# S5 states through two PSUM banks, readouts in trace order, an earlier 1/rms and tables split by use, in a two-layer hybrid block

## The chip, the core and the metric

The kernel runs on one core of a Trainium2 chip. The metric is the device time of one execution in microseconds (us). A core has five engines with an instruction stream each: PE (TensorE, matrix products and transposes), DVE (VectorE), ACT (ScalarE), POOL (GpSimd) and SP (SyncE, which here only issues transfers). The engines run side by side and wait for one another through semaphores. PE writes into PSUM, a small memory of eight banks; the other engines empty these banks into SBUF, the working memory.

## The reference, cut to what matters

512 latent tokens and 256 context tokens, 1024 channels wide, go through two layers. Each layer is

```
h     = modulate(x, sh1, sc1);  hc = modulate(ctx, ...)    # shift and scale from silu(c) @ w_mod[l]
proj  = h @ w_in[l]             # keys, values, latent keys, u of S5, queries, three gates
ya    = grouped-query attention (8 heads of 64, 2 key heads), rms-normed q and k, rotary
yc    = latent attention: cq = rms_norm(proj[..., C_Q]); qc = cq @ c_w_qb; keys, values = ckv @ c_w_kvb
ys    = S5: states s[t] = abar * s[t-1] + bbar @ u[t] (complex, 32 groups of 64 states, forward and
        backward over the tokens), y = Re(C s) + d * u, gelu, gated linear unit
mix   = (sigmoid(g0)*(ya@Wa) + sigmoid(g1)*(ys@Ws) + sigmoid(g2)*(yc@Wc)) @ w_out
x     = layer_norm(alpha*x + g1*mix);  then a squared-ReLU MLP of 4096 with a modulation and a norm
```

The context tokens take the same way in layer 0; in layer 1 only their keys, values and S5 states are needed. All results are float32.

## The kernel before

**Products.** A float32 operand is split into a high part, rounded to the matrix format, and a low part (the rest). A product is three matmuls: high x high, low x high, high x low (`mm3`, L167 to L169). For weights a DMA brings the raw tile (`wr`), ACT casts the high part `wh` (L151), and DVE subtracts to get `wl` (L124). These three lines carry most of PE's time.

**The stages of a layer**, in time: the modulated input; projections, which run beside a part of the gates (sigmoids of `h @ w_in`, blocks of 128 columns); the chunk states of S5; attention of both kinds, beside which a "filler" runs (gates, the S5 readouts, the last gates); the merge of the three branches; `w_out` and the norm; the MLP. Beside the MLP of layer 0 run the tables and the modulation of layer 1. Beside the merge of layer 0 runs the rest of layer 0's own modulation (`mods(l, (5,))`): 16 loads `wm` of 256 KB, which DVE multiplies and adds into `acc` (L309), a sum by PE, and a small DMA.

**S5.** The 768 tokens are cut into 96 chunks of 8. From the constants of a layer, `s5_tables` makes small matrices per group: `gb`, which PE transposes (L580) and which gives Q (input of a chunk to its end state), P (`pt`, state at a chunk's start to the chunk's outputs) and M (input to output within a chunk). They are written to memory (`Qd`, `Pd`, `Md`) and loaded again. `s5_states` forms the end states of all chunks: for each of 16 pairs of groups, a load `qp`, four matmuls `b<-u,qp` (L1027) into one PSUM bank, then three copies into `slots`, forward states and backward ones in turned order (L1030 to L1032). GpSimd then scans over the 96 chunks (L1040 to L1043). `s5_readout` takes eight quarter-steps of four groups each: loads `m` and two `qp` and, every second time, `u`; GpSimd copies the states of the groups to `bsl` (L1060 to L1063); PE does M times u (L1070) and P times states (L1073); ACT takes the bank to `y`. `m` and `bsl` have one buffer each, `qp` three in layer 0 and four in layer 1.

**Latent queries.** `compress(hf, ms)` makes the six 128-row blocks of `cq` for one half of the tokens, with the sum of squares in `acc`; `queries(hf)` sums `acc` over rows on PE (L832), takes 1/rms (`rstd_of`, L648 and L649), and multiplies by `w_qb`, with 1/rms as a factor when ACT empties the bank (L643).

**What sets the order.** The Python code is traced once. Generators that run side by side are drawn from in turn, by weights (`merge`, `mixed`); every instruction gets a priority by when it was traced, `later(gen, d)` adds to it, and a list scheduler with a simulated time line then fixes the order in each engine's stream. An engine runs its stream strictly in that order. All DMAs are issued from one queue, SP's (L78), in one order as well. `issue_after(i)` keeps what is traced inside it behind the instruction `i` on i's engine. A tile pool with n buffers hands out the same memory after n tiles, and the next user waits for the last reader of the old one.

Of the kernel before, what the change touches and what calls it, by code (L numbers as in the profile page):

```python
# [21 lines left out]
P = 128  # L22
# [47 lines left out]
class Block:  # L70
# [36 lines left out]
    def later(self, gen, d, behind=()):  # L107

        while True:
# [10 lines left out]
            yield v  # L120

# [404 lines left out]
    def s5_tables(self, pool, l, engs, G):  # L526
# [5 lines left out]
        for q in range(16 // G):  # L532
            tt = engs[q % len(engs)].tensor_tensor
# [30 lines left out]
            tt(out=gb[:, :, 1], in0=m1, in1=m2, op=ALU.add)
            yield 2.0
            pt = self.t(pool, [P, N, 2, 8, 16], F32, "pt")
            tt(out=m1, in0=pw(s["qr"]), in1=ch(ct[:, 0]), op=ALU.mult)
            tt(out=m2, in0=pw(s["qi"]), in1=ch(ct[:, 1]), op=ALU.mult)
            tt(out=pt[:, :, 0], in0=m1, in1=m2, op=ALU.subtract)
            nci = self.t(pool, [P, N, 16], F32, "nci")  # L570
            nc.vector.tensor_scalar(out=nci, in0=ct[:, 1], scalar1=-1.0, scalar2=None, op0=ALU.mult)
            tt(out=m1, in0=pw(s["qr"]), in1=ch(nci), op=ALU.mult)
            tt(out=m2, in0=pw(s["qi"]), in1=ch(ct[:, 0]), op=ALU.mult)
            tt(out=pt[:, :, 1], in0=m1, in1=m2, op=ALU.subtract)
# [9 lines left out]

            cb = self.t(pool, [P, N, 2, 2, 16], F32, "cb")
            nc.gpsimd.memset(cb, 0.0)
            for dr in range(2):
                hp = slice(dr * 64, dr * 64 + 64)
                nc.gpsimd.tensor_copy(cb[hp, :, 0, dr, :], ct[hp, 0])
                nc.gpsimd.tensor_copy(cb[hp, :, 1, dr, :], nci[hp])  # L590
# [110 lines left out]
    def projections(self, l, hT, pool, tp, per):  # L701
# [127 lines left out]
        def queries(hf):  # L829
# [5 lines left out]
            r = self.rstd_of(ps[:, :, 0], (8, nt), 96 * EPS)  # L835
# [23 lines left out]
        yield from compress(1, range(3))  # L859
        yield from queries(0)  # L860
        yield from compress(1, range(3, 6))
        yield from queries(1)
# [151 lines left out]
    def s5_states(self, sp, l, slots):  # L1014
# [4 lines left out]
        for gp in range(16):  # L1019
# [4 lines left out]
            ps = self.bank([P, 2, 2, NCH], which="gate")  # L1024
# [5 lines left out]
            nc.scalar.copy(sv[fw, :, :, 1:96], ps[fw, :, :, 0:95])  # L1030
            nc.scalar.copy(sv[bw, :, :, 1:33], ps[bw, :, :, 31::-1])
# [14 lines left out]
    def s5_readout(self, sp, l, slots):  # L1046
# [5 lines left out]
        for q in range(8):  # L1052
# [13 lines left out]
            for g in range(4):  # L1066
                if g % 2 == 0:
                    pt = self.t(sp, [P, 2, 2, P], F32, "qp")
                    self.dma(out=pt.rearrange("p g r c -> p (g r c)"), in_=self.Pd[l, q * 2 + g // 2])
# [471 lines left out]
```

## Time and profile before

| | |
|---|---|
| median of 3 runs | 2761.7 us (2759.91 to 2764.09) |
| the profiled execution | 2761.72 us, of which the instructions span 2759.9 us |
| mean granted clock of PE in it | 0.962 of full speed |
| busy: PE, DVE, ACT, POOL | 2570.2, 1794.7, 1197.2, 1167.4 us |
| DMA | 395.40 MB, mean 143 GB/s |

Line numbers (L1027) are lines of the kernel that the profile belongs to; the changed kernel's are 5 to 12 higher behind the first new function. A row of a group, "L1030 ACT COPY slots<-b x32: 787/817/866, 395.2 to 1942.3", gives engine, operation, what is written from what (by the names of the program), count, the shortest, median and longest duration in ns, and the first and last start in us. A row of the time line, "406.61 2.02 PE L1027 MATMUL b<-u,qp ... x8 [1.05 <-ACT slots L1032]", gives start and duration in us and in brackets how long the engine had stood still before it, and what ended that. A row of the waits, "PE b L1027 <- ACT slots L1032: 19.6, 24, 1.7", gives who waited for whom: the sum in us, the number of waits, the longest. In the table of stretches each engine has its busy time and its number of instructions; PEclk is the granted clock of PE, the mean over the stretch. A row of the transfers, "qp<-Qd SPq DMA_DIRECT2D x32, 256.0 KB, 3.0", ends with the median us from issue to landing.

In the order's listings below, a row is one instruction of one engine's stream: line, operation, output<-inputs with the program's names and buffer numbers, the shape, and a count where equal rows follow each other.

### The profile page before, as it was taken

To read this page: it belongs to the slowest core of one execution; us is meant where nothing else is said; L and a number is where in the kernel's file an instruction comes from. 1 tells how busy PE (TensorE), PEld (TensorE's weight loads), DVE (VectorE), ACT (ScalarE), POOL (GpSimd) and SP (SyncE) were. 2 spreads that over 40 slices of the span, in tenths; PEclk is the share of its full clock that TensorE was granted. 3 is DMA by queue.
4 is the path that set the end of the run, shared out by engine and by line. 5 is a ranking of instruction groups with operands and counts; after the bars stand their busy time and mean duration, and the time that the engine had idled before them with its cause. 6 is when DMAs were issued, how large, how long until landed. Compare 5 with 4: busy or idle time off the path is not lost.

```text
span 2759.9 us, 45140 instructions
## 1 busy us (share of the span) xinstructions
PE 2570.2 (93%) x16128; PEld 2380.6 (86%) x16128; DVE 1794.7 (65%) x3338; ACT 1197.2 (43%) x2420; POOL 1167.4 (42%) x1698
## 2 busy tenths in 40 slices
PE   7999998999899989999999988998998989799997
PEld 4989898999899878999999988997877868688886
DVE  7998535777778678456668574455766757844345
ACT  4333367655543235132322234457654633533332
POOL 2378313870202577445446361310785004722224
PEclk9989998999999999999999999999999989899999
DMA  8665666333464535334535256457433445433332
GB/s 242 203 191 154 173 180 178 109 98 114 156 197 127 197 124 172 98 101 141 151 111 157 90 160 175 118 152 209 131 100 118 136 149 176 137 108 106 107 100 84
DMA packets 485312, 395.40 MB, mean 143 GB/s; under 512 B 103624, under 2 KB 413128, under 8 KB 485088
## 3 DMA queue, kind: packets, MB, share of 16 engines
q1 hardware_dynamic: 485088, 392.53, 47.2%
q8 instruction: 127, 2.08, 0.3%
q14 instruction: 97, 0.79, 0.1%
HBM read 326.87 MB, written 70.67 MB: 144 GB/s over the span
## 4 chain that ended last, share of the span: by engine, by line
PE 62%; DVE 10%; POOL 10%; DMA 8%; ACT 4%; issue 4%; SPq 1%; POOLq 0%; DVEq 0%; ACTq 0%
PE b L168 17%; PE b L169 17%; PE b L167 17%; PE sc L872 3%; DVE acc L309 2%; DVE wl L124 2%; PE b L891 2%; DMA wm<-w_mod 2%; POOL slots L1043 1%; POOL sc L1040 1%; POOL sc L1042 1%; POOL sc L1041 1%; DMA wr<-w_in 1%; PE b L904 1%; PE b L903 1%
## 5 line engine op out<-in xcount | busy, mean ns | idle before, releaser
L151 ACT CAST wh<-wr 128x512 fp32r<-128x512 f32 (+1 forms) x672 | 410.0, 619 | 739.8 <-PE b L168 278.5
L124 DVE TENSOR_TENSOR wl<-wr,wh 128x512 fp32r<-128x512 f32 (+2 forms) x612 | 486.7, 807 | 293.4 <-ACT wh L151 282.7
L167 PE MATMUL b<-h,wh 128*128 128x384 f32 (+2 forms) x1712 | 597.4, 350 | 18.8 <-ACT wh L151 11.0
L169 PE MATMUL b<-h,wl 128*128 128x384 f32 (+2 forms) x1712 | 593.1, 347 | 7.8 <-DVE wl L124 7.6
L168 PE MATMUL b<-h,wh 128*128 128x384 f32 (+2 forms) x1712 | 594.7, 348 | 5.5 <-POOL h L393 4.4
L168 PE MATMUL b<-wl,a 128*128 128x256 f32 (+1 forms) x1460 | 446.9, 310 | 10.5 <-DVE wl L124 9.1
L169 PE MATMUL b<-wh,a 128*128 128x256 f32 (+1 forms) x1460 | 444.9, 308 | 0.0
L167 PE MATMUL b<-wh,a 128*128 128x256 f32 (+1 forms) x1460 | 438.4, 309 | 6.1 <-ACT a L643 3.8
L167 PEld LDWEIGHTS b<-h,wh 128*128 128x128 f32 x1712 | 327.6, 192 | 38.0 <-ACT wh L151 12.3
L169 PEld LDWEIGHTS b<-h,wl 128*128 128x128 f32 x1712 | 326.9, 191 | 27.9 <-DVE wl L124 12.2
L168 PEld LDWEIGHTS b<-h,wh 128*128 128x128 f32 x1712 | 327.4, 191 | 24.3 <-POOL h L393 6.0
L168 PEld LDWEIGHTS b<-wl,a 128*128 128x128 f32 x1460 | 280.0, 192 | 25.9 <-DVE wl L124 11.6
L167 PEld LDWEIGHTS b<-wh,a 128*128 128x128 f32 x1460 | 276.0, 192 | 22.5 <-ACT a L643 3.9
L1201 POOL TENSOR_TENSOR acc<-acc,tmp 128x256 f32<-128x256 f32 (+1 forms) x160 | 170.4, 1068 | 285.9 <-DVE tmp L1200 272.7
L169 PEld LDWEIGHTS b<-wh,a 128*128 128x128 f32 x1460 | 280.0, 192 | 12.5
L309 DVE SCALAR_TENSOR_TENSOR acc<-wm,silu,acc 128x512 f32<-128x512 f32 x236 | 194.6, 845 | 29.3 <-DMA wm<-w_mod 26.5
L1226 POOL TENSOR_TENSOR sq<-r 128x384 f32<-128x384 f32 (+2 forms) x102 | 99.0, 972 | 239.3 <-ACT r L1224 226.5
L1200 DVE TENSOR_TENSOR tmp<-b,bc 128x256 f32<-128x256 f32 (+1 forms) x160 | 77.2, 484 | 168.8 <-PE b L169 151.3
L894 DVE TENSOR_TENSOR pt<-b,pt 128x512 fp32r<-128x512 f32 x208 | 141.9, 685 | 33.2 <-ACT pt L893 31.7
L875 DVE TENSOR_REDUCE mx<-sc 128x1 f32<-128x768 f32 (+1 forms) x160 | 134.1, 844 | 34.3 <-PE sc L872 33.4
L167 PE MATMUL b<-a,wh 128*128 128x384 f32 (+1 forms) x384 | 131.2, 369 | 16.6 <-ACT a L1152 11.8
L878 ACT ACTIVATE p<-sc,mx 128x768 f32<-128x768 f32 (+1 forms) x160 | 131.5, 823 | 34.4 <-PE b L891 19.4
(377 smaller groups left out, 5138.8 us busy)
## 6 DMA issues: line engine op xcount, KB each, us to landing
wr<-w_in SPq DMA_DIRECT2D x84, 512.0 KB, 4.2
wr<-w_up SPq DMA_DIRECT2D x76, 512.0 KB, 5.1
wr<-w_down SPq DMA_DIRECT2D x74, 512.0 KB, 3.8
wm<-w_mod SPq DMA_DIRECT2D x64, 512.0 KB, 4.7
wm<-w_mod SPq DMA_DIRECT2D x64, 256.0 KB, 2.9
wr<-w_out SPq DMA_DIRECT2D x26, 512.0 KB, 3.8
gd<-sg SPq DMA_DIRECT2D x48, 192.0 KB, 3.1
sg<-gd SPq DMA_DIRECT2D x24, 384.0 KB, 3.3
```

Source lines behind the costliest of these rows:

```text
L124: self.nc.vector.tensor_tensor(out=out, in0=src, in1=hi, op=ALU.subtract)
L151: self.nc.scalar.copy(h, raw[:, j0:j0 + jj])
L167: mm(ps, lhsT=a[0], rhs=b[0], start=start, stop=False)
L168: mm(ps, lhsT=a[0], rhs=b[1], start=False, stop=False)
L169: mm(ps, lhsT=a[1], rhs=b[0], start=False, stop=stop)
L309: i = nc.vector.scalar_tensor_tensor(out=acc, in0=w, scalar=s, in1=acc, op0=ALU.mult, op1=ALU.add)
L872: nc.tensor.matmul(sc[:, n0:n1], lhsT=q[:, qs], rhs=k[:, n0:n1], start=i == 0, stop=i == len(passes) - 1)
L875: nc.vector.reduce_max(out=mx, in_=sc[:, 0:nkey], axis=AX.X, negate=True)
L878: nc.scalar.activation(pt, sc[:, 0:nkey], AF.Exp, bias=mx, accum_out=sm)
L894: nc.vector.tensor_tensor(out=lo, in0=ps, in1=hi, op=ALU.subtract)
L1201: nc.gpsimd.tensor_tensor(out=r[t][:, cs], in0=r[t][:, cs], in1=tmp, op=ALU.add)
L1226: nc.gpsimd.tensor_tensor(out=sq, in0=rl, in1=rl, op=ALU.mult)
```

## The change

1. `s5_states`: the PSUM bank of a pair of groups is in turn from the pool "gate" (one bank) and "pv" (three), and the three copies into `slots` run in turn on ScalarE and on VectorE, where ScalarE did all.
2. `s5_readout`: the twelve matmuls of each step are traced inside `placed()`, which holds them behind the PE instruction that was traced last before them. The scheduler can no longer move them forward past it.
3. `queries` is cut in two: `rms(hf)`, the sum and the 1/rms, and the rest. `rms(0)` is called when one block of the second half's `compress` is done, where it was called when three were.
4. `s5_tables`: the products for `bb` and `gb` always run on VectorE and those for `pt` always on GpSimd; before, each step of the loop ran all of them on one engine, the engines in turn. `gb` and `pt` are worked out in place, with one auxiliary tile each (`mm`, `mp`) where two were shared; `cb` is made before `pt` where it was made at the step's end. The loops in layer 0 take eight steps, those of layer 1 sixteen.

```diff
+    def placed(self):
+        pe = [i for i in self.nc.cur_bb.bb.instructions[-4000:] if i.engine == mybir.EngineType.PE]
+        return self.tc.issue_after(pe[-1])
...
-    def s5_tables(self, pool, l, engs, G):
+    def s5_tables(self, pool, l, G):
...
-            tt = engs[q % len(engs)].tensor_tensor
+            tt = nc.vector.tensor_tensor
...
+            nc.gpsimd.memset(cb, 0.0)
+            tt = nc.gpsimd.tensor_tensor
+            m2 = self.t(pool, [P, N, 8, 16], F32, "mp")
+            pt = self.t(pool, [P, N, 2, 8, 16], F32, "pt")
+            tt(out=pt[:, :, 0], in0=pw(s["qr"]), in1=ch(ct[:, 0]), op=ALU.mult)
...
-        def queries(hf):
+        def rms(hf):
             ps = self.bank([P, nt, 2], which="tr")
...
-            r = self.rstd_of(ps[:, :, 0], (8, nt), 96 * EPS)
+            return self.rstd_of(ps[:, :, 0], (8, nt), 96 * EPS)
+
+        def queries(hf, r):
...
         yield from compress(0, range(6))
-        yield from compress(1, range(3))
-        yield from queries(0)
+        yield from compress(1, range(1))
+        r0 = rms(0)
+        yield from compress(1, range(1, 3))
+        yield from queries(0, r0)
         yield from compress(1, range(3, 6))
-        yield from queries(1)
+        yield from queries(1, rms(1))
...
-            ps = self.bank([P, 2, 2, NCH], which="gate")
+            ps = self.bank([P, 2, 2, NCH], which=("gate", "pv")[gp % 2])
...
-            nc.scalar.copy(sv[fw, :, :, 1:96], ps[fw, :, :, 0:95])
-            nc.scalar.copy(sv[bw, :, :, 1:33], ps[bw, :, :, 31::-1])
-            nc.scalar.copy(sv[bw, :, :, 33:96], ps[bw, :, :, 95:32:-1])
+            copy = (nc.scalar.copy, nc.vector.tensor_copy)[gp % 2]
+            copy(sv[fw, :, :, 1:96], ps[fw, :, :, 0:95])
+            copy(sv[bw, :, :, 1:33], ps[bw, :, :, 31::-1])
+            copy(sv[bw, :, :, 33:96], ps[bw, :, :, 95:32:-1])
...
+            with self.placed():
+                for g in range(4):
...
-            drain(self.s5_tables(sq, 0, (self.nc.vector, self.nc.gpsimd), 2))
+            drain(self.s5_tables(sq, 0, 2))
```

How this moves instructions is seen in the engines' streams. First PE's stream in layer 0 before the change, where the chunk states begin (L1027; `stk` is a stack of query heads that PE transposes at L696, `sc` are attention's scores, L872):

```order
L1027 MATMUL b_4997<-u_4973,qp_4995 128x96 x4
L696 MATMUL b_4757<-identr_71,stk_4752 128x128 x4
L1027 MATMUL b_5007<-u_4973,qp_5005 128x96 x4
L696 MATMUL b_4765<-identr_71,stk_4752 128x128 x4
L1027 MATMUL b_5019<-u_5015,qp_5017 128x96 x4
L872 MATMUL sc_5726<-k_2497,q_5711 128x256
L872 MATMUL sc_5774<-k_2497,q_5711 128x256
L696 MATMUL b_4776<-identr_71,stk_4773 128x128 x4
```

And the same place after it (the states are L1037, the scores L882):

```order
L882 MATMUL sc_5841<-k_2497,q_5722 128x512
L882 MATMUL sc_5841<-k_2497,q_5722 128x256
L1037 MATMUL b_4987<-u_4973,qp_4985 128x96 x4
L1037 MATMUL b_5007<-u_4973,qp_5005 128x96 x4
L1037 MATMUL b_5029<-u_5015,qp_5027 128x96 x4
L1037 MATMUL b_5039<-u_5015,qp_5037 128x96 x4
L1037 MATMUL b_5049<-u_5015,qp_5047 128x96 x4
```

Before, transposes and scores stood between the pairs of groups; after, 13 of layer 0's 16 pairs follow one another, behind the first scores of attention.

Next, PE's stream at a readout in layer 0's attention before the change (L903 and L904 are attention's products with the values, `vt`, L891 its transposes; `u` and `m` at L1070 and `bsl` and `qp` at L1073 make up the readout):

```order
L903 MATMUL b_9963<-pt_9922,vt_8839 128x256
L1073 MATMUL b_10310<-bsl_10305,qp_10311 128x96 x2
L1070 MATMUL b_10310<-u_10277,m_10303 128x96
L1073 MATMUL b_10310<-bsl_10305,qp_10311 128x96 x2
L1070 MATMUL b_10310<-u_10277,m_10303 128x96
L1073 MATMUL b_10310<-bsl_10305,qp_10319 128x96 x2
L1070 MATMUL b_10310<-u_10277,m_10303 128x96
L1073 MATMUL b_10310<-bsl_10305,qp_10319 128x96
L904 MATMUL b_9963<-pt_9923,vt_8839 128x256
```

After the change, PE's stream at the end of layer 0's attention (values L913 and L914, readout L1082 and L1085):

```order
L913 MATMUL b_10124<-pt_10120,v_8840 128x256
L914 MATMUL b_10124<-pt_10121,v_8840 128x256
L1082 MATMUL b_10148<-u_10004,m_10141 128x96
L1085 MATMUL b_10148<-bsl_10143,qp_10149 128x96 x2
...
L1085 MATMUL b_10148<-bsl_10143,qp_10157 128x96 x2
L1082 MATMUL b_10176<-u_10169,m_10167 128x96
L1085 MATMUL b_10176<-bsl_10171,qp_10177 128x96 x2
```

The last readout (`b_10310`) stood in the middle of an attention step; now the second (`b_10148`) begins behind the very last product with the values, and the third (`b_10176`) and all the others follow it directly. Two sums of the modulation stand among them, then come 48 matmuls of gates, then the merge. In layer 1 it is the same with six readouts.

Last, SP's queue after the change at that place (`m_10195` and `m_10221` belong to the fourth and fifth readout, `qp` are their P matrices, `Yd` the outputs, `wm` the modulation's loads):

```order
L78 DMA m_10195<-Md_90 128x512
L78 DMA qp_10231<-Pd_91 128x512
L78 DMA Yd_98<-y_10175 128x384
L78 DMA wm_11564<-w_mod 128x512
L78 DMA wm_11678<-w_mod 128x512
L78 DMA wm_11768<-w_mod 128x512
L78 DMA wm_11833<-w_mod 128x512
L78 DMA qp_10239<-Pd_91 128x512
L78 DMA wm_11923<-w_mod 128x512
L78 DMA m_10221<-Md_90 128x512
```

Before, all `wm` loads of this modulation stood behind the last `m`, among the merge's weights; now 15 of the 16 stand between the loads of the readouts.

More of the change, by code (lines that the diff above doesn't have):

```diff
@@ new lines, in s5_tables @@
+            for dr in range(2):
+                hp = slice(dr * 64, dr * 64 + 64)
+                nc.gpsimd.tensor_copy(cb[hp, :, 0, dr, :], ct[hp, 0])
+                nc.gpsimd.tensor_copy(cb[hp, :, 1, dr, :], nci[hp])
+            tt = nc.gpsimd.tensor_tensor
+            m2 = self.t(pool, [P, N, 8, 16], F32, "mp")
+            pt = self.t(pool, [P, N, 2, 8, 16], F32, "pt")
+            tt(out=pt[:, :, 0], in0=pw(s["qr"]), in1=ch(ct[:, 0]), op=ALU.mult)
+            tt(out=m2, in0=pw(s["qi"]), in1=ch(ct[:, 1]), op=ALU.mult)
@@ L583, in s5_tables @@
                 self.dma(out=self.Qd[l, q * G + g], in_=qt.rearrange("p i c -> p (i c)"))
[L585 to L590, printed above, removed]
             yield 2.0
@@ L1065, in s5_readout @@
             ps = self.bank([P, 4, nn], which="gate")
[L1066 to L1069, printed above, removed]
-                nc.tensor.matmul(ps[:, g], lhsT=M[:, g], rhs=u[:, 4 * (q % 2) + g, n0:],
-                                 start=True, stop=False)
-                for ri in range(2):
-                    nc.tensor.matmul(ps[:, g], lhsT=pt[:, g % 2, ri, :], rhs=bst[:, ri, g], start=False,
-                                     stop=ri == 1)
+            with self.placed():
+                for g in range(4):
+                    if g % 2 == 0:
+                        pt = self.t(sp, [P, 2, 2, P], F32, "qp")
+                        self.dma(out=pt.rearrange("p g r c -> p (g r c)"), in_=self.Pd[l, q * 2 + g // 2])
+                    nc.tensor.matmul(ps[:, g], lhsT=M[:, g], rhs=u[:, 4 * (q % 2) + g, n0:],
+                                     start=True, stop=False)
+                    for ri in range(2):
+                        nc.tensor.matmul(ps[:, g], lhsT=pt[:, g % 2, ri, :], rhs=bst[:, ri, g], start=False,
+                                         stop=ri == 1)
             nc.scalar.copy(y, ps)
@@ L1353, in tables @@
                 yield 1.0
-                yield from self.s5_tables(sq, 0, (self.nc.vector, self.nc.gpsimd), 2)
+                yield from self.s5_tables(sq, 0, 2)
             drain(self.later(tables(), 300))
```

25 lines of the change are left out of this document (11 added, 14 removed).

## The prediction

> **What bounds the kernel now.** I read the page first: its busy shares and its chain.
>
> ```profile
> span 2759.9 us, 45140 instructions
> PE 2570.2 (93%) x16128; PEld 2380.6 (86%) x16128; DVE 1794.7 (65%) x3338; ACT 1197.2 (43%) x2420; POOL 1167.4 (42%) x1698
> PE 62%; DVE 10%; POOL 10%; DMA 8%; ACT 4%; issue 4%; SPq 1%; POOLq 0%; DVEq 0%; ACTq 0%
> ```
>
> TensorE is the bound, so a change pays only where PE stands still or runs at half clock. I then cut the span into the stretches that the change touches.
>
> ```profile
> core 0: us, PE busy (x) PEld busy (x) DVE busy (x) ACT busy (x) POOL busy (x), PEclk, DMA share, GB/s
> 100.00:320.00 220.00, 208.75 (x1415) 203.85 (x1414) 188.24 (x312) 84.59 (x183) 146.82 (x140) 0.94 0.58 171
> 320.00:345.00 25.00, 20.57 (x149) 20.15 (x148) 10.90 (x19) 7.95 (x17) 0.86 (x1) 0.86 0.77 230
> 395.00:460.00 65.00, 52.48 (x323) 47.12 (x322) 32.78 (x71) 55.02 (x116) 4.19 (x13) 0.82 0.69 196
> 405.60:426.10 20.50, 16.10 (x74) 14.91 (x74) 3.84 (x10) 14.91 (x33) 0.00 (x0) 0.50 0.79 228
> 690.00:785.00 95.00, 85.95 (x648) 81.49 (x647) 71.25 (x142) 53.35 (x128) 24.38 (x23) 1.00 0.47 149
> 785.00:810.00 25.00, 20.89 (x113) 20.22 (x112) 16.16 (x25) 8.59 (x14) 0.00 (x0) 0.86 0.63 208
> 810.00:950.00 140.00, 131.41 (x730) 126.77 (x729) 117.36 (x238) 48.30 (x80) 52.99 (x50) 0.96 0.50 158
> 1870.00:1945.00 75.00, 62.51 (x446) 56.35 (x445) 40.76 (x75) 61.77 (x125) 6.07 (x12) 0.93 0.72 211
> 2085.00:2112.00 27.00, 16.71 (x95) 15.41 (x94) 12.02 (x23) 8.50 (x19) 18.62 (x47) 0.75 0.19 54
> 2112.00:2195.00 83.00, 80.72 (x592) 74.96 (x591) 62.56 (x124) 46.76 (x113) 14.18 (x12) 1.00 0.53 158
> 2195.00:2245.00 50.00, 34.62 (x160) 28.71 (x160) 28.81 (x52) 22.49 (x46) 0.00 (x0) 0.76 0.41 126
> ```
>
> I call "loss" the length less PE busy times PEclk. It is 23.8 us in the tables and projections of layer 0 (100:320), 7.3 where its queries start (320:345), 22.0 and 16.9 in the chunk states (395:460, 1870:1945). The end of layer 0's attention with the merge behind it loses 9.1 + 7.0 + 13.8 = 29.9, layer 1's 14.5 + 2.3 + 23.7 = 40.5. That is all the change can win, 140 us. The waits name the causes.
>
> ```profile
> PE b L1027 <- ACT slots L1032: 19.6, 24, 1.7
> PE b L1073 <- POOL bsl L1063: 9.7, 1, 9.7
> PE b L580 <- POOL gb L564: 5.3, 2, 3.7
> ```
>
> **Part 1: chunk states through two banks.**
>
> ```profile
> 406.61 2.02 PE L1027 MATMUL b<-u,qp 128*128 128x96 f32 x8 [1.05 <-ACT slots L1032]
> 1903.88 1.13 PE L1027 MATMUL b<-u,qp 128*128 128x96 f32 x8 [1.00 <-ACT slots L1032]
> L1030 ACT COPY slots<-b x32: 787/817/866, 395.2 to 1942.3; 64x380 f32<-64x380 f32 x32
> L1031 ACT COPY slots<-b x32: 367/376/398, 396.1 to 1943.1; 64x128 f32<-64x128 f32 x32
> L1032 ACT COPY slots<-b x32: 605/622/657, 396.3 to 1943.3; 64x252 f32<-64x252 f32 x32
> L407 DVE COPY xT<-b x6: 670/676/692, 25.2 to 65.8; 128x512 f32<-128x512 f32 x6
> qp<-Qd SPq DMA_DIRECT2D x32, 256.0 KB, 3.0
> ```
>
> Today one bank passes from PE (1.13 us, 2.02 at half clock) to three ACT copies (0.82 + 0.38 + 0.62 = 1.82 us): 3 us a group, 16 groups a layer. Eight groups (14.6 us a layer) now go to VectorE, which is busy only 33 of 65 us there. The DVE price for strided slots isn't in the trace: scaled from L407 by elements it is 1.0 us a group, at worst ACT's 1.8. Either fits beside the ACT group, so a pair takes 1.13 + 1.82 + 0.2 = 3.1, or 1.55 us a group. But the order now puts 13 of layer 0's groups one behind another on PE, with three buffers for loads that land after 3.0 us while DMA already moves 196 GB/s there: I take 2.0 us a group. Loss in layer 0: 13 x (2.0 - 1.1) + 4 for the other three = 16, a gain of 6. Layer 1 has four buffers and scores between: I take 5. **Term -11.** Bounds: PE-bound at 1.13 us a group (3 us lost a layer) gives -33; unchanged pace with nothing between the groups, 13 x 2.0 + 4 = 30, gives +8, and about +5 in layer 1: +13. Behind a DVE slot copy wait the row maxima and the splits of the first units, some 1 us each, hidden by the gates, which may now start at once.
>
> The clock: from 405.6 to 426.1 it is 0.50 although no single wait was longer than 1.7 us. The Trainium skill ("TensorE: Matmul & The Clock Gate", HAM oscillation) asks only that PE-idle gaps stay under about 3.4 us; by that rule this stretch would have kept its clock and part 1 could win about 10 us less in layer 0. The trace disagrees, and I go by the trace.
>
> **Part 2: readouts in trace order.** What each is made of:
>
> ```profile
> 739.55 1.56 POOL L1060 COPY bsl<-slots 64x768 f32<-64x768 f32 x1 [7.20 <-PE b L1073]
> 741.16 0.62 POOL L1062 COPY bsl<-slots 64x256 f32<-64x256 f32 x1
> 741.72 1.06 POOL L1063 COPY bsl<-slots 64x512 f32<-64x512 f32 x1
> 2132.79 0.33 PE L1070 MATMUL b<-u,m 128*128 128x64 f32 x2
> 2135.36 0.61 PE L1073 MATMUL b<-bsl,qp 128*128 128x64 f32 x4
> m<-Md SPq DMA_DIRECT2D x16, 256.0 KB, 3.7
> ```
>
> Today the eight readouts lie between attention steps, so the turn-round of their single buffers (`m`, `bsl`) is covered. In the new order seven of layer 0 and six of layer 1 follow the last PV matmul, with nothing between them but two small sums of the modulation. PE then waits for each. A readout takes PE 2.7 us in layer 1 (2132.79 to 2135.97, less 0.44 of a transpose), and with 96 columns for 64 in layer 0 at most 3 x 1.13 = 3.4 (the row of L1027); I take 3.1. `m` is free after about 85% of it; then come issue 0.3 and landing 3.7: a period of 6.6 us in layer 0, 6.3 in layer 1. The other buffer needs 3.1 + 3.3 (the three copies): no longer.
>
> Layer 1: 2.7 + 5 x 6.3 = 34 at full clock. PE idles 3.6 of 6.3 us, a busy share of 43%; the stretch from 405.6 did 16.10 x 0.50 = 8.1 us of full-clock work in 20.5, 39%, and had lost the clock. So some of these run at half; by 2.02 against 1.13 they need 4.9, a period of 8.2. I take 7.2, and 1 us for residual rows that load beside the first: 40. Of this 16 us is work that stood elsewhere: loss 24.
>
> Layer 0 has the modulation's loads in the SP queue between those of `m`, 15 of its 16:
>
> ```profile
> wm<-w_mod SPq DMA_DIRECT2D x64, 256.0 KB, 2.9
> 800.03 2.74 DVE L309 SCALAR_TENSOR_TENSOR acc<-wm,silu,acc 128x512 f32<-128x512 f32 x4 [1.39 <-DMA wm<-w_mod]
> 845.12 1.34 PE L167 MATMUL b<-a,wh 128*128 128x384 f32 x5 [3.80 <-ACT a L128]
> ```
>
> With two `wm` buffers a load costs (2.9 + 2 x 0.69)/2 = 2.1 us: 16 take 34 us; the single accumulators between its two halves I estimate at 6 (two small DMAs, taken at the 2.9 of a large one). SP runs in order, so `m` stands behind them, and PE meets both sums before readouts 4 and 6: readout 6 starts near 43, the last ends near 53; beside the loads of `m` and `qp` that is over 200 GB/s, so I take 57. Work in it: 7 x 3.1 = 22. Loss 35. In return the merge loses these 32 DVE operations: the wait of 3.80 and its half clock behind it, 5.5.
>
> What else goes: the 9.7 us wait for `bsl` and its half clock, and the waits between readouts. What is late next: the last gate block (behind the readouts; I put 1.7 us for its start at half clock, an estimate) and the merge, since its weights reuse memory read by the last `bsl` copy. Its start loses 7.0 today in layer 0 and I keep it. In layer 1 today:
>
> ```profile
> 2225.55 0.58 PE L904 MATMUL b<-pt,v 128*128 128x256 f32 x1 [4.68 <-DVE pt L894]
> 2237.45 0.79 PE L167 MATMUL b<-a,wh 128*128 128x512 f32 x1 [5.61 <-ACT a L1152]
> ```
>
> The first goes (the weights that filled DVE come later), the second I put at 8 with its clock. The attention's last unit has no filler: 4 us a layer.
> Layer 0 after: 4 + 35 + 1.7 + 7 + (13.8 - 5.5) = 56 against 29.9: **+26**. Layer 1: 2 (readout 1) + 4 + 24 + 1.7 + 8 = 40 against 40.5: **-1**. Bounds: layer 0's chain 3.1 + 6 x 6.6 = 43 if the modulation holds nothing, 66 if a load costs its whole 2.9 us (16 x 0.8 = 12 more, partly under the last readouts): -14 to +9; layer 1's 34 to 47.
>
> **Part 3: 1/rms a block sooner.**
>
> ```profile
> L167 PE MATMUL b<-wh,a 128*128 128x256 f32 (+1 forms) x1460 | 438.4, 309 | 6.1 <-ACT a L643 3.8
> 326.72 1.20 ACT L643 ACTIVATE a<-b,rs 128x256 f32<-128x256 f32 x3
> ```
>
> In the whole run PE's first product waits 3.8 us for L643, all of it here: L643 scales the queries' input by 1/rms and stood on ACT behind a weight cast. With the factor ready, it can stand ahead. Of the 7.3 us I take 4, since the cast's load lands as late: **-4** (0 to -7). Layer 1 has no such wait.
>
> **Part 4: tables by use.** `gb` (what PE transposes) always on DVE, `pt` always on POOL.
>
> ```profile
> L543 DVE TENSOR_TENSOR bb<-s5b,cr x12: 171/190/810, 81.7 to 1491.8; 128x32 f32<-128x32 f32 x8, 128x64 f32<-128x64 f32 x4
> L543 POOL TENSOR_TENSOR bb<-s5b,cr x12: 237/392/4699, 113.1 to 1466.3; 128x32 f32<-128x32 f32 x8, 128x64 f32<-128x64 f32 x4
> ```
>
> The large products stay 48 on each engine; 24 small ones (four steps of six) move to DVE: 24 x 0.2 = 5 us more on an engine busy 188 of 220 us, and some 10 fewer on POOL. The waits for `gb` from POOL (5.3 us) should go; splits of weights may wait longer on DVE. **-2** (-10 to +8). In layer 1's tables MLP matmuls hide either way: 0.
>
> **Sum.** -11 + 26 - 1 - 4 - 2 = +8 on this execution's 2761.7 us (span 2759.9 plus 1.8), which is the median of the runs: 2770.
>
> **Rivals.**
> 1. Faster: the two banks feed PE at its own pace in both layers (1.13 us a group, loads keeping up). -33 in place of -11 gives 2748. It ends below "before" once a group takes less than about 1.6 us. For it: DVE half idle, the ACT wait is the named one. Against: 196 to 211 GB/s there already. Chance 0.22.
> 2. No change: the modulation's loads don't hold `m`, layer 0's chain is 43 and the sum -6: 2756, at the edge of 0.2%, which is about what a measurement can tell. Against: SP is one queue in order. Chance 0.18.
> 3. Slower still: half clock all through the chains. Layer 1's is 4.9 + 5 x 8.2 + 1 = 47 (+7), layer 0's +4, two gates +3.5: 2784. For it: 43% busy. The skill's rule on gaps, with 3.6 us against 3.4, would say the same. Chance 0.15.
> The forecast, 2763 to 2779 by itself, has 0.45.
>
> **Numbers.** Faster: rival 1 and a part of 2, 0.27. Same: most of 2 and the forecast's low end, 0.23. Slower: 0.50. The range reaches to rival 1 and past rival 3, for the slower pace of groups: 2748 to 2793.
>
> **What would show it.** After the last PV matmul, PE busy under 50% for 40 to 60 us in each layer, L1082 waiting for `m<-Md`; `wm` loads between them; no wait of L1085 for POOL of 9 us; L1037 groups 1.5 to 2.2 us apart. Wrong if the chain's period is near 3 us, or the states' stretches lose under 5 us each.

## The result, and the profile after

The changed kernel takes 2846.97 us (median of 4 runs, 2845.5 to 2854.01), beside 2762.01 for the kernel before: 1.0311 times as long, 95% interval 1.0298 to 1.0324, 85 us more. The profiled execution took 2854.01 us, 7 more than the median. Its page, first span and busy shares, then the chain's shares by engine:

```profile
span 2852.2 us, 45158 instructions
PE 2610.6 (92%) x16128; PEld 2410.2 (85%) x16128; DVE 1843.5 (65%) x3458; ACT 1175.5 (41%) x2372; POOL 1166.6 (41%) x1626
PE 65%; DVE 14%; DMA 8%; POOL 4%; issue 4%; ACT 3%; SPq 1%; POOLq 0%; DVEq 0%; ACTq 0%
```

PE's busy time grew by 40 us though it has the same 16128 matmuls; the granted clock fell from 0.962 to 0.946. The rest is standing still. By stretches (length, then busy time of PE, PEld, DVE, ACT and POOL with the number of instructions, granted clock, DMA):

```profile
core 0: us, PE busy (x) PEld busy (x) DVE busy (x) ACT busy (x) POOL busy (x), PEclk, DMA share, GB/s
100.00:328.00 228.00, 199.43 (x1341) 193.76 (x1340) 191.23 (x324) 82.97 (x178) 153.98 (x117) 0.92 0.55 163
328.00:350.00 22.00, 21.25 (x157) 21.09 (x156) 8.01 (x13) 8.62 (x18) 0.86 (x1) 1.00 0.67 196
410.00:457.70 47.70, 38.12 (x216) 35.33 (x215) 23.80 (x46) 25.92 (x53) 1.46 (x5) 0.75 0.87 266
690.00:780.00 90.00, 78.02 (x522) 67.92 (x521) 77.94 (x170) 57.75 (x143) 4.35 (x5) 0.98 0.23 70
780.00:846.00 66.00, 36.87 (x179) 30.30 (x178) 30.01 (x34) 6.73 (x13) 23.64 (x20) 0.67 0.58 189
846.00:865.00 19.00, 11.14 (x48) 10.50 (x48) 2.08 (x4) 2.50 (x5) 0.00 (x0) 0.77 0.35 113
865.00:1023.00 158.00, 149.11 (x856) 146.83 (x857) 111.13 (x225) 51.46 (x83) 52.12 (x48) 0.97 0.49 152
1950.00:2004.00 54.00, 42.28 (x273) 39.02 (x271) 30.94 (x57) 29.18 (x60) 3.24 (x7) 0.81 0.64 192
2267.00:2311.00 44.00, 29.12 (x145) 28.37 (x143) 0.43 (x1) 2.23 (x6) 10.34 (x10) 0.57 0.57 175
2311.00:2327.00 16.00, 8.76 (x26) 6.50 (x25) 4.99 (x8) 5.23 (x10) 0.00 (x0) 0.71 0.83 255
```

Loss is again length less PE busy times PEclk. The seven readouts behind layer 0's attention (780:846) lose 41 us, six in layer 1 (2267:2311) 27, the gates behind them (846:865, 2311:2327) 10 each. Layer 0's tables (100:328) lose 44.5 where they lost 23.8. The queries' start (328:350) loses 0.8 where it lost 7.3. The chunk states lose 19 and 20, as before (22 and 17). The waits of PE, largest of those that changed (sum, number, longest):

```profile
PE b L1082 <- DMA m<-Md: 28.6, 8, 5.9
PE b L172 <- ACT a L1164: 15.5, 3, 7.8
PE b L593 <- DVE gb L565: 10.5, 4, 5.2
PE b L602 <- ACT qt L595: 9.7, 3, 6.4
PE b L334 <- DVE acc L314: 8.5, 2, 6.2
```

ACT's `slots`, 19.6 us before, is gone from the head of the list, and `m` has taken its place. PE's wait for `gb`, 5.3 us for GpSimd before, is now one of 10.5 us for VectorE.

### The profile page after: what moved, and what is told of

It reads as the page before. It is cut to its first block, busy times and chain, and to the rows that moved or that the text cites. A ratio compares the mean times of both kernels' runs of the same rounds, so it can differ in the third digit from the quotient of the medians.

```text
span 2852.2 us, 45158 instructions
## 1 busy us (share of the span) xinstructions
PE 2610.6 (92%) x16128; PEld 2410.2 (85%) x16128; DVE 1843.5 (65%) x3458; ACT 1175.5 (41%) x2372; POOL 1166.6 (41%) x1626
## 4 chain that ended last, share of the span: by engine, by line
PE 65%; DVE 14%; DMA 8%; POOL 4%; issue 4%; ACT 3%; SPq 1%; POOLq 0%; DVEq 0%; ACTq 0%
PE b L172 18%; PE b L173 18%; PE b L174 18%; PE sc L882 3%; PE b L901 2%; DVE acc L314 2%; DMA wm<-w_mod 2%; DVE wl L129 2%; PE b L914 1%; DVE mx L885 1%; PE b L913 1%; DVE pt L904 1%; SPq L78 1%; PE b L1085 1%; DVE p L890 1%
## 5 line engine op out<-in xcount | busy, mean ns | idle before, releaser
L156 ACT CAST wh<-wr 128x512 fp32r<-128x512 f32 x672 | 410.2, 619 | 769.2 <-PE b L174 295.0
L129 DVE TENSOR_TENSOR wl<-wr,wh 128x512 fp32r<-128x512 f32 (+1 forms) x612 | 482.9, 801 | 346.8 <-ACT wh L156 340.3
L314 DVE SCALAR_TENSOR_TENSOR acc<-wm,silu,acc 128x512 f32<-128x512 f32 x236 | 205.7, 894 | 47.1 <-DMA wm<-w_mod 32.5
L904 DVE TENSOR_TENSOR pt<-b,pt 128x512 fp32r<-128x512 f32 x208 | 141.6, 683 | 19.8 <-ACT pt L903 18.3
L1071 POOL COPY bsl<-slots 64x768 f32<-64x768 f32 (+1 forms) x16 | 21.8, 1360 | 314.5 <-PE b L1085 314.3
```

Of the source, the lines that this page charges most:

```text
L129: self.nc.vector.tensor_tensor(out=out, in0=src, in1=hi, op=ALU.subtract)
L156: self.nc.scalar.copy(h, raw[:, j0:j0 + jj])
L314: i = nc.vector.scalar_tensor_tensor(out=acc, in0=w, scalar=s, in1=acc, op0=ALU.mult, op1=ALU.add)
L904: nc.vector.tensor_tensor(out=lo, in0=ps, in1=hi, op=ALU.subtract)
```

## The experiments

The runs are numbered in the order in which they ran. Each is timed beside the kernel before on the same chip; costs in us are worked out from the ratios, on 2762 us. "Alone" means the kernel before with that part of the change.

**The four parts, one at a time.** First the holding of the readouts alone:

```diff
-            for g in range(4):
+            with self.placed():
+                for g in range(4):
```

Run 1:

> The kernel before with the second part alone: the readouts' matmuls held in trace order, all else as before. Theory A (the fixed order of the readouts is the main loss: the two chains of waits for m at half clock, and the gates behind them, cost 51 us more than before in layer 0 and 10 in layer 1, by the losses of the two traces): 2762 + 61 = 2823, between 2810 and 2835. Rival B (the chains cost what the prediction put, +26 and -1, and the rest of the 85 us comes from the other three parts): 2787. Rival C (the chains only take up time that the merge behind them would lose anyway): within 5 us of 2762.

Measured: 2832.67 us, ratio 1.0256 (1.0238 to 1.0273): 71 us. Theory A had the size nearly right, B and C fall. Stretches of this run (the columns as above): the last of layer 0's attention, its seven readouts, the gates, the merge; then the same four of layer 1, with six readouts.

```profile
690.00:766.00 76.00, 66.39 (x452) 57.73 (x453) 66.02 (x136) 48.23 (x113) 4.34 (x5) 1.00 0.25 73
766.00:838.00 72.00, 39.40 (x172) 32.84 (x171) 30.96 (x35) 6.45 (x13) 22.91 (x20) 0.60 0.52 171
838.00:854.40 16.40, 8.87 (x48) 8.23 (x48) 1.77 (x3) 2.44 (x6) 0.00 (x0) 0.91 0.42 144
854.40:1012.40 158.00, 149.48 (x853) 147.60 (x854) 110.95 (x226) 51.54 (x83) 52.00 (x48) 0.97 0.49 151
2158.00:2244.00 86.00, 76.83 (x535) 67.88 (x533) 73.09 (x148) 53.92 (x129) 6.80 (x6) 1.00 0.24 71
2244.00:2288.40 44.40, 29.32 (x143) 28.39 (x142) 0.43 (x1) 2.20 (x6) 10.32 (x10) 0.54 0.57 174
2288.40:2304.40 16.00, 7.17 (x24) 5.49 (x24) 4.99 (x8) 5.13 (x10) 0.00 (x0) 0.71 0.82 261
2304.40:2405.00 100.60, 98.88 (x427) 81.41 (x428) 71.86 (x96) 40.26 (x68) 24.91 (x16) 0.98 0.56 179
```

The losses are 9.6, 48.4, 8.3 and 13.0 us in layer 0, then 9.2, 28.6, 10.9 and 3.7 in layer 1.

The tables alone:

```diff
-            tt = engs[q % len(engs)].tensor_tensor
+            tt = nc.vector.tensor_tensor
...
+            tt = nc.gpsimd.tensor_tensor
```

Run 2:

> The kernel before with the fourth part alone: gb on VectorE, pt on GpSimd. Theory A (the tables cost layer 0's projections 18 us, by the losses of 24.2 and 42.1 us in the two traces between 100 us and the queries): 2762 + 18 = 2780, between 2774 and 2786. Rival B (the delay in layer 0 is taken up behind the projections, as GpSimd's scan ends at 612 and 614 us in both kernels): 2762, within 4. Rival C (the split helps, as the prediction had it): 2760 or less.

Measured: 2770.35, ratio 1.0025 (1.0012 to 1.0039): 7 us, between A and B. PE's waits in the tables of this run:

```profile
PE b L588 <- DVE gb L560: 8.2, 3, 5.2
PE b L597 <- ACT qt L590: 6.7, 2, 4.6
```

Before, they were 5.3 us for GpSimd's `gb` and 2.4 for `qt`. So the wait for `gb`, which was to go, moved to VectorE and grew. The tables lose 43 us where they lost 24; of these 19 us more, 12 are made up before the end.

The states alone:

```diff
-            ps = self.bank([P, 2, 2, NCH], which="gate")
+            ps = self.bank([P, 2, 2, NCH], which=("gate", "pv")[gp % 2])
...
+            copy = (nc.scalar.copy, nc.vector.tensor_copy)[gp % 2]
```

Run 3:

> The kernel before with the first part alone: chunk states through two banks, copies by ScalarE and VectorE in turn. Here 10 of layer 0's 16 pairs of groups follow one another on PE and the readouts are spread over attention. Theory A (the states gain what their stretch of the two traces shows, the sum of losses from the states to the scan's start 20.9 + 16.3 before and 20.1 + 20.1 after, and little beside): 2762, within 6. Rival B (the pairs run at PE's pace where no other part disturbs them): 2735. Rival C (as the prediction had it, -11): 2751.

Measured: 2764.03, ratio 0.9999 (0.999 to 1.0009). Theory A holds, B and C fall. The states' stretches of this run, PE's wait in the first of them, and (of the changed kernel) VectorE's first slot copy, shortest, median and longest in ns:

```profile
384.00:444.70 60.70, 50.25 (x302) 46.76 (x301) 29.27 (x58) 33.46 (x68) 3.47 (x8) 0.75 0.64 185
1876.00:1930.00 54.00, 44.54 (x290) 40.83 (x289) 30.84 (x58) 30.78 (x63) 4.52 (x8) 0.81 0.66 197
```

```profile
PE b L1027 <- DMA qp<-Qd: 6.3, 4, 2.6
```

```profile
L1041 DVE COPY slots<-b x16: 779/797/821, 431.6 to 2000.7; 64x380 f32<-64x380 f32 x16
```

VectorE copies at ScalarE's price. The stretches end 13 and 14 us sooner, but they lose 23 and 18 us as before: the wait for the copies has become one for `qp`, and the scores and transposes that once stood between the groups are done later.

The changed kernel without the holding:

```diff
-            with self.placed():
+            if True:
```

Run 4:

> The kernel after without the second part: the readouts' matmuls free to move, all else as after. Theory A (that part alone costs 61 us): 2847 - 61 = 2786, between 2774 and 2798. Rival B (that part costs 25, the other three 60): 2822. Rival C (the other three parts gain, and the placement loses more than 85 us): below 2762.

Measured: 2778.29, ratio to before 1.0052 (1.0038 to 1.0067), 72 us under the changed kernel by the two ratios, as far as the first run lies over the kernel before (71). Theory A holds.

The 1/rms alone:

```diff
+        yield from compress(1, range(1))
+        r0 = rms(0)
+        yield from compress(1, range(1, 3))
```

Run 11:

> The third part alone, 1/rms a block sooner. Theory A (as predicted: PE's wait for L643 in layer 0 goes, 4 us): 2764 - 4 = 2760. Rival B (the wait goes, but attention or the merge behind give it back, as they gave back the states' gain): within 2 of 2764. Rival C (the earlier sum takes a bank or a place from the second half's compression, by the 13 us that all but the second part cost together less 6 for the tables): 2771.

Measured: 2762.54, ratio 1.0001 (0.9993 to 1.001). That is rival B's number, but not its reason, for the wait did not go. ScalarE and PE at the queries' start in this run:

```profile
325.15 0.62 ACT L151 CAST wh<-wr 128x512 fp32r<-128x512 f32 x1 [1.93 <-DMA wr<-w_qb]
325.68 1.20 ACT L643 ACTIVATE a<-b,rs 128x256 f32<-128x256 f32 x3
326.20 0.58 PE L167 MATMUL b<-wh,a 128*128 128x256 f32 x1 [3.99 <-ACT a L643]
```

L643 still stands behind the weight cast, which waits for its load, and PE waits 4.0 us where it waited 3.8.

**Why the held readouts cost 71 us.** The modulation's loads, taken out from among them:

```diff
-            self.dma(out=M, in_=self.Md[l]...)
+            self.mlast = self.dma(out=M, in_=self.Md[l]...)
...
-  self.later(self.mods(l, (5,), kk=1, eager=True), 100)
+  self.later(self.mods(l, (5,), kk=1, eager=True), 100, (self.mlast.ins,))
```

Run 5:

> The readouts held in trace order alone (as in the first run, 2833), and the modulation's wm loads held behind the last load of m in SP's queue. In layer 0 no wm load and no sum stands among the readouts any more. Theory A (half of layer 0's chain is the modulation's: its 72 us fall to 47, seven readouts of 6.7 us as in layer 1, of which the merge takes back 5): 2833 - 20 = 2813. Rival B (the loads of m and the half clock alone make the chain, the wm loads lie beside): within 5 of 2833. Rival C (the merge takes back all of it, since 16 loads now meet the weights' casts): 2833 or more with a chain of 47.

Measured: 2821.0, ratio 1.0208 (1.0192 to 1.0224): 13 us less than run 1, between A and B. Its readouts of layer 0, and PE's waits from them to the merge:

```profile
766.70:819.60 52.90, 35.68 (x168) 33.22 (x166) 3.16 (x5) 3.23 (x7) 18.27 (x18) 0.62 0.49 149
```

```profile
PE b L1077 <- DMA m<-Md: 15.3, 6, 3.9
PE b L173 <- ACT y L1082: 7.3, 1, 7.3
```

The chain falls from 72 to 53 us, and some of that comes back as a longer wait of the gates for the bank (`y`). So the modulation is 19 us of that chain and 13 of the whole; the larger part stays, at a clock of 0.62. Theory A's 47 us took 6.7 a readout; layer 1's readouts in the changed kernel are 7.4 apart (rows further down), and seven of these make the 52 that were found.

The readouts held, but traced earlier:

```diff
-                merge((self.attention(...), ...), (filler(), (170.0, 100.0)[l]))
+                merge((self.attention(...), ...), (filler(), (260.0, 160.0)[l]))
```

Run 6:

> The readouts held in trace order, and the filler (gates, readouts, gates) drawn faster beside attention, by the weights 260 and 160 for 170 and 100: the eight readouts now stand between 0.59 and 0.80 of attention's products with the values in layer 0 and between 0.53 and 0.78 in layer 1. Theory A (what costs is that they stood behind attention, not that they are held): the chains go, some waits in attention's last fifth without filler come, 2762 + 8 = 2770, between 2760 and 2782. Rival B (a readout that can't move away from a late load costs its wait wherever it stands: 7 readouts of 4 us in each layer): 2815.

Measured: 2763.24, ratio 0.9999 (0.9988 to 1.001). Theory A, and better than its 2770: not the holding costs the time but the place that it holds. In the changed kernel the names told it already: the readouts from `b_10148` on have higher numbers than `b_10124`, the last product with the values, so they are traced behind attention, and only the scheduler had brought them forward. The same two numbers in the changed kernel:

Run 12:

> The changed kernel whole, with the filler's weights 260 and 160 for 170 and 100, so that the readouts are held in trace order amid attention. Theory A (the readouts' place behind attention is 71 us of the 85): 2847 - 71 = 2776, between 2768 and 2784. Rival B (with the other three parts the held readouts cost some of it still, for the last gates' and readouts' loads come beside the states' banks from pv): 2795.

Measured: 2766.6, ratio to before 1.0018 (1.0008 to 1.0029): 81 us under the changed kernel, rather more than A had; rival B falls.

**The states with half their loads.**

The kernel leaves out half of Q and uses the first group's matrices for both groups.

```diff
-            self.dma(out=q.rearrange("p g r c -> p (g r c)"), in_=self.Qd[l, gp])
+            self.dma(out=q[:, 0].rearrange("p r c -> p (r c)"), in_=self.Qd[l, gp, :, 0:256])
...
-                    nc.tensor.matmul(ps[:, gl, ri, :], lhsT=q[:, gl, ri, :], ...)
+                    nc.tensor.matmul(ps[:, gl, ri, :], lhsT=q[:, 0, ri, :], ...)
```

Run 8:

> The first part alone (as in the third run, 2764), with half of each pair's Q left out: a load qp of 128 KB for 256 KB, and the first group's matrices used for both groups. Theory A (the wait for the bank has become one for qp, and the stretch's loss of 23 us in layer 0 is its landing at half clock): the loss falls to 12 in layer 0 and by 4 in layer 1, and the whole to 2764 - 13 = 2751. Rival B (the states end sooner, but what they gain is given back by attention, which ends when it did): within 4 of 2764. Rival C (not the load but the order, ten pairs with nothing between them, sets the pace through the copies): the states' stretch as long as in the third run.

Measured: 2762.91, ratio 0.9999 (0.9985 to 1.0013). Layer 0's states in this run:

```profile
384.00:438.50 54.50, 42.70 (x304) 39.69 (x302) 27.79 (x56) 31.22 (x64) 3.49 (x8) 0.87 0.59 165
```

The loss falls to 17 us, where theory A had 12, so the load was part of it, and still nothing comes through at the end: rival B.

**The tables: four attempts.** In place, the engines in turn:

```diff
-            tt = nc.vector.tensor_tensor
+            tt = (nc.vector, nc.gpsimd)[(q + l) % 2].tensor_tensor
...
-            tt = nc.gpsimd.tensor_tensor
```

Run 7:

> The tables of the changed kernel (in place, a separate auxiliary tile for pt, cb made before pt), but with all products of a step on one engine, the engines in turn, as in the kernel before. Theory A (the loss in layer 0's tables, 18 us, comes from the split by use: pt on GpSimd in every step beside a busy VectorE, where single products took up to 13 us, and VectorE then waits 13 us for GpSimd's rotary product): as the kernel before, 2762, within 4. Rival B (the products in place, which wait for one another, or cb standing ahead of pt on GpSimd, are the cost): as the second run, 2769.

Measured: 2791.17, ratio 1.0101 (1.0084 to 1.0118), worse than both theories. PE's longest wait in its tables is for ScalarE's `qt`:

```profile
PE b L596 <- ACT qt L589: 18.1, 7, 7.0
```

So the split by use is not the cost. It takes back most of the 28 us that the rest of the new tables costs.

P stored later (the products for `pt` stand behind the Q stores, and a step's P is stored in the next step):

```diff
+            with self.tc.issue_after(last.ins):      # last: the store of Q
+                store()                              # P of the step before
...
-                self.dma(out=self.Pd[l, q * G + g], in_=pt[...])
+            held.append((q, pt))
```

Run 9:

> The fourth part alone (as in the second run, 2770), with the stores of P (Pd<-pt) held in SP's queue behind the next step's stores of Q, so that SP no longer stands on GpSimd's pt. Theory A (the cost of the tables is SP's: it waits 32 us for pt in six waits, 12.3 the longest, while weights and Qd<-qt stand behind it, and ScalarE's single qt and then PE wait for those): 2770 - 8 = 2762, within 4, and no wait of SP for pt over 3 us. Rival B (the cost is VectorE's waiting for GpSimd's rotary product, 13 us, behind pt in GpSimd's stream): within 3 of 2770.

Measured: 2775.56, ratio 1.0047 (1.0034 to 1.006). SP's wait for `pt` is gone from its list, and nothing is gained, rather 6 us lost beside run 2, outside rival B's range too. Theory A finds no support. The edit changes more than the wait that it treats: `pt` now stands behind PE's transposes, and GpSimd waits 18.0 us once for PE before it fills `cb` (0.7 in run 2).

The rotary product on VectorE:

```diff
-        nc.gpsimd.tensor_tensor(out=t1, in0=xn, in1=tabs[0], op=ALU.mult)
+        (nc.vector, nc.gpsimd)[self.cl].tensor_tensor(out=t1, in0=xn, in1=tabs[0], op=ALU.mult)
```

Run 10:

> The fourth part alone, with the rotary embedding's first product on VectorE in layer 0, where GpSimd had it. VectorE then no longer waits for GpSimd there. Theory A (SP's wait for pt is the cost): within 3 of 2770, or some us more for VectorE's added products. Rival B (VectorE's 13 us of waiting for GpSimd's t are the cost): 2762, and the loss of layer 0's tables back near 24.

Measured: 2775.62, ratio 1.0047 (1.0033 to 1.0061). VectorE's wait for GpSimd's rotary product is gone, and the time isn't: rival B falls too. What both attempts treated is in these rows: SP's and VectorE's waits in the run with the tables alone, then a time line row of GpSimd in the changed kernel, then one product on GpSimd in the tables of both kernels (count, busy us, mean ns), the tables alone first and the kernel before second.

```profile
SPq L78 <- POOL pt L582: 31.5, 6, 11.5
DVE t L688 <- POOL t L684: 13.5, 3, 6.6
```

```profile
197.40 13.07 POOL L585 TENSOR_TENSOR pt<-qr,nci 128x512 f32<-128x512 f32 x1 [1.47 <-DVE nci L571]
```

```profile
L580 POOL TENSOR_TENSOR pt<-qr,nci 128x512 f32<-128x512 f32 x8 | 33.0, 4129 | 2.5 <-DVE nci L566 2.5
```

```profile
L572 POOL TENSOR_TENSOR mm<-qr,nci 128x512 f32<-128x512 f32 x4 | 4.5, 1113 | 0.2
```

The same product takes 4.1 us on average for 1.1. Three of its eight make the difference, with 3.5, 8.7 and 13.1 us in run 2; the others take 1.5 to 1.6.

Last, the second auxiliary tile for `pt`, and in another run for `gb`:

```diff
+            m1 = self.t(pool, [P, N, 8, 16], F32, "mp1")     # the other run: "mm1", for gb
-            tt(out=pt[:, :, 0], in0=pw(s["qr"]), ...)
+            tt(out=m1, in0=pw(s["qr"]), ...)
-            tt(out=pt[:, :, 0], in0=pt[:, :, 0], in1=m2, op=ALU.subtract)
+            tt(out=pt[:, :, 0], in0=m1, in1=m2, op=ALU.subtract)
```

Run 13:

> The fourth part alone, but pt is not worked out in place: a second auxiliary tile (mp1) takes the first product on GpSimd, as mm1 did before, so that pt's single buffer is wanted only at the third product. Theory A (the products in place cost the time: pt's first product stands on GpSimd until the store Pd<-pt of the step before has landed, 21 us in five waits, 8.2 the longest, and all behind it on GpSimd with it): 2770 - 8 = 2762. Rival B (gb in place does it, which PE's transposes of the step before hold): within 3 of 2770. Rival C (GpSimd's products are slow beside a busy VectorE, wherever they write): within 3 of 2770, with the next run there as well.

Run 14:

> The fourth part alone, but gb is not worked out in place: a second auxiliary tile (mm1) on VectorE, pt as in the change. Theory A (pt in place is the cost): within 3 of 2770. Rival B (gb in place is the cost: VectorE's first product waits for PE's transposes two steps before): 2762. Rival C (neither): within 3 of 2770.

Measured: 2820.99 and 2824.16, ratios 1.0215 (1.0201 to 1.0229) and 1.022 (1.0201 to 1.0238). All the theories fail. Either tile costs nearly the same, 52 and 54 us over run 2. That suggests a cause in what both have in common, one more tile in the tables' pool, rather than in where the product is written, but no run shows it. It wasn't followed further, and the two runs say nothing on the products in place.

**All but the tables, with the readouts amid attention**, then without the holding, then also with the old weights:

```diff
 states through two banks, 1/rms sooner, tables as before
-  (filler(), (170.0, 100.0)[l])
+  (filler(), (260.0, 160.0)[l])      # runs 15 and 16
+            with self.placed():      # run 15 alone
```

Run 15:

> The first three parts (states through two banks, readouts held, 1/rms sooner), the tables as in the kernel before, and the filler's weights 260 and 160. Theory A (the parts add up: each of the three alone, with the readouts amid attention, was within 2 us of 2763, and the tables account for what the twelfth run lost): 2762, within 4. Rival B (the parts help each other once nothing stands behind attention and the tables are as before): 2755 or less. Rival C (the states' banks from pv and the held readouts hinder each other): 2768 or more.

Run 16:

> As the fifteenth run (states through two banks, 1/rms sooner, tables as before, filler's weights 260 and 160: 2753), but with the readouts' matmuls free to move. Theory A (holding them costs nothing amid attention and brings nothing, the 9 us come from the earlier filler with the earlier scan): 2753, within 4. Rival B (held readouts stand better, since they no longer interrupt attention's steps): 2760 or more.

Run 17:

> The first and the third part alone, readouts free, tables and the filler's weights as before. Theory A (the gain of the fifteenth run needs the filler drawn faster, since an earlier end of the states is otherwise given back by attention): within 3 of 2763. Rival B (the two parts together gain by themselves, 9 us, and neither the weights nor the holding matter): 2753.

Measured: 2752.79, ratio 0.9961 (0.9947 to 0.9975); not held 2766.16, 1.0016 (1.0006 to 1.0026); old weights too 2764.19, 1.001 (1.0001 to 1.0019). The first is faster than both kernels, by 0.4% beside the kernel before; run 15 comes out as its rival B had it, run 16 as its rival B, run 17 as its theory A. Beside parts 1 and 3, holding the readouts amid attention gains 15 us (0.9961 for 1.0016); with the new weights but without these parts it gained nothing (run 6); held behind attention, the readouts cost 71. The profiled executions of runs 15 and 16 lie 21 us apart (2747.09 and 2768.5). From layer 1's scan to the end of attention, the held version first, then the free one:

```profile
1929.00:2089.00 160.00, 152.61 (x899) 133.41 (x900) 117.79 (x224) 93.23 (x206) 137.76 (x377) 0.99 0.41 118
2089.00:2214.00 125.00, 111.20 (x799) 101.32 (x797) 95.71 (x184) 72.42 (x167) 18.39 (x16) 0.99 0.45 136
```

```profile
1935.00:2093.80 158.80, 146.93 (x850) 128.21 (x848) 113.82 (x216) 89.34 (x198) 136.67 (x377) 0.97 0.39 116
2093.80:2235.50 141.70, 125.70 (x850) 115.00 (x850) 101.84 (x193) 76.11 (x175) 18.92 (x17) 0.92 0.41 124
```

The held version loses 24 us here, the free one 42. In the free one, GpSimd's last step of the scan and PE at the layer's first readout:

```profile
2093.52 0.32 POOL L1048 TENSOR_TENSOR slots<-slots,sc 128x64 f32<-128x64 f32 x1
2096.06 1.11 PE L1078 MATMUL b<-bsl,qp 128*128 128x64 f32 x4 [7.74 <-POOL bsl L1068]
```

PE comes to the first readout before the scan is over: it stands from 2088.3 us until the scan's last states are copied to `bsl`, and then runs at half clock until 2104 (0.50 from 2096 on). In run 15 the scan's last step starts at 2088.45 and the first readout at 2091.65, without a wait. The same wait is in the kernel before (9.7 us, the row in the prediction), in run 17 (8.9) and in run 6 (11.2, though held). So neither the new weights alone (run 16) nor the holding with them (run 6) removes it; with the earlier states and the earlier 1/rms as well (run 15), the first readout comes to stand behind the end of the scan. How much of the 18 us it makes, with its half clock, no run takes apart. The tables, too, can be sized here: run 12 is run 15 with the new tables, and their ratios, 1.0018 and 0.9961, lie 0.57% or 16 us apart. Runs 4 and 17, with the old weights and the readouts free, differ by the tables alone as well: 0.42% or 12 us.

## Why the prediction was wrong, step by step

The direction was right and the place of the largest term too. Its size was not, and the gains that were to pay for most of it (parts 1, 3 and 4) did not come: the sum was +8, the result +85. Alone, the four parts make 0 + 71 + 0 + 7 = 78 of it; the rest lies in the tables, which cost more beside the other parts.

- **Part 2, forecast +25, alone +71.** This is the step that failed: "Layer 0 after: 4 + 35 + 1.7 + 7 + (13.8 - 5.5) = 56". By the first run's rows its terms are 9.6 (attention's end, for 4), 48.4 (the chain, for 35), 8.3 (the gates, for 1.7) and 13.0 (the merge, for 15.3), 79 in all, 23 more. That PE would wait for `m` between the readouts was right; the chain was mis-sized. It was given 57 us, with bounds of 43 and 66, and took 72 alone and 66 beside the other parts. Run 5 divides the miss: without the modulation's loads the chain took 53 us where the sum had 43, and the loads added 19 where it had 14. The first 10 us are the clock. The sum and its bounds took each readout at full clock; in run 5 PE was busy for 35.7 us at a mean clock of 0.62, which is just the 22 us of work in the sum, stretched. Here are PE's readouts of layer 1 in the changed kernel, the first matmuls of three in a row:

```profile
2283.67 0.66 PE L1082 MATMUL b<-u,m 128*128 128x64 f32 x2 [2.70 <-issue]
2291.08 0.66 PE L1082 MATMUL b<-u,m 128*128 128x64 f32 x2 [2.06 <-DMA m<-Md]
2298.57 0.66 PE L1082 MATMUL b<-u,m 128*128 128x64 f32 x2 [2.13 <-DMA m<-Md]
```

  They are 7.4 us apart, as the 7.2 that the prediction took for layer 1, and PE works 5.3 of them (2291.08 less 2.06 less 2283.67) where 2.7 was the full-clock price. There the chain's 44 us answer to the 40 forecast. In run 1 its loss is 28.6 us for 24; the rest of that end's error is attention's last step, 9.2 for 6 (2 + 4), and the gates, 10.9 for 1.7, less the merge, 3.7 for 8. Rival 3, half clock all through, was the right picture at too low a price: it gave layer 0 only 4 us for it, where run 5 has 10. One of the signs named did not come for the same reason: PE was to be busy for under 50% of the chains, and was for 56 and 66% (36.87 of 66 us, 29.12 of 44), since at half clock the same work takes twice as long.
- **The modulation in SP's queue** was read rightly from the order. SP's own time line between two loads of `m` in the changed kernel:

```profile
782.70 0.38 SPq L78 DMA_DIRECT2D m<-Md  x1
784.56 7.38 SPq L78 DMA_DIRECT2D wm<-w_mod  x3
793.36 0.38 SPq L78 DMA_DIRECT2D m<-Md  x1
```

  Three loads of `wm` hold SP for 7.4 us, 2.5 each, where 2.1 was taken. With 13 us of 71 (run 5) it is the smaller part of the cost. Rival 2, that these loads hold nothing, falls.
- **Where the rest of the 71 is.** The losses at the two ends of attention grew by 49 us in layer 0 (79 for 29.9) and by 11 in layer 1 (52.4 for 41.5, with the 1.0 that its merge lost before), by the rows of run 1. The last 11 us do not show in these stretches; the measure takes PE's modelled busy time as work.
- **Part 1, forecast -11, alone 0.** The pace came out right, as seven pairs in a row of the changed kernel show,

```profile
439.58 12.60 PE L1037 MATMUL b<-u,qp 128*128 128x96 f32 x56 [2.87 <-DMA qp<-Qd]
```

  1.8 us a pair where 2.0 was taken. That was luck in part: the 2.0 stood for loads that land late, and the trace shows PE working for these 12.6 us without a pause, at a granted clock of 0.52. The copies' price was near the upper bound (0.80 us for the first one, as on ScalarE). What failed is the loss put beside it, 16 us where run 3 has 23, for a clock of 0.75 that was not in that sum, and the account itself: before, PE had worked between the groups, so a shorter stretch was no shorter program. In run 3 the states end 13 us sooner, and PE's last product with the values of layer 0 starts at 790.6 us, where it started at 788.9 before. Run 8 shows that not even a smaller loss there reached the end.
- **Part 3, forecast -4, alone 0.** The step "With the factor ready, it can stand ahead" failed: in run 11 L643 still stands behind the weight cast, and the wait is 4.0 us for 3.8. In the changed kernel this stretch loses 0.8 us for 7.3, but there the tables bring the queries 8 us later, and which of the two removed the wait isn't shown.
- **Part 4, forecast -2, alone +7, beside the other parts +12 to +16.** The step priced 24 small products on VectorE, and took GpSimd's products at their old duration. One kind of them became four times as long in the mean. The wait for `gb` that was to go (5.3 us) became one for VectorE (8.2 in run 2), and that for `qt` grew from 2.4 to 6.7. What makes these two late stays open: run 10 shows that VectorE's wait for GpSimd is not the cause by itself, and run 9 gives no sign that SP's is.

What part 1 gains had a cover that I did not name: attention behind it ended no sooner. A faster filler does not lift it by itself either, since run 16 has one and stays at 2766; only with the readouts held as well (run 15) did the whole get shorter.

## What to carry to other kernels

An edge that fixes an instruction in trace order is worth what its place in trace order is worth: look first where the generator's weights have traced it, and what would be left there to fill PE's waits. A chain of short PE bursts between loads into a single buffer is to be priced at half clock from the start; here such chains ran at 0.54 to 0.67. Before a readout is moved forward, look where the scan that feeds it ends. A stretch that gets shorter because filler left it has gained nothing; count the loss, not the length.

## What was not expected of the hardware

**The clock did not come back between short waits.** In layer 1 of the changed kernel PE waited 5.9 us for `m` until 2275.6 us, and from then to 2311 the clock was 0.50, though PE worked 5.3 us between waits of 2.1 to 2.7 (the rows above). In layer 0's chunk states it was 0.50 from 445.0 to 452.2 us, with PE busy for 7.15 of 7.18 us by its modelled ends. The Trainium skill ("TensorE: Matmul & The Clock Gate", HAM oscillation) puts the limit at PE-idle gaps of some 3.4 us. The drop in layer 1 agrees with that, by the 5.9 us; that the clock then stays low through shorter gaps is more than this limit says.

**GpSimd products of 13 us beside a busy VectorE**, for 1.5 to 1.6 us in five of run 2's eight. The Trainium skill ("SBUF — State Buffer", SBUF: two separate sides) describes a port pair that the two engines share under an exclusive lock, which the one that started holds for its whole instruction. The trace fits that in kind, since VectorE worked without a pause beside the product of 13.07 us; but a single VectorE instruction there lasts 0.2 to 1.4 us, so a wait of 12 would have to span many of them; no run here took VectorE's work away to show it.
